# Grouping the small products of two scans by the part of the array they use

## The chip, the cores and the metric

One core of one Trainium2 chip runs the whole program in one launch. The metric is device time in microseconds (us), the median of several executions. The profile is one more execution, taken by the hardware profiler. Engines are called PE (TensorE's matmuls), PEld (its weight loads), DVE (VectorE), ACT (ScalarE), POOL (GpSimd) and SP (SyncE, which issues the transfers).

## The reference

Three layers run one after the other on a sequence of 2048 tokens with 1024 features, all in float32. Each of the first two projects its input, runs a chunked linear attention with four heads, multiplies by gates, projects back and normalises. Only the attention of these two layers is touched by the change.

```python
# layer 0, chunks of 64 tokens, 4 heads, dk = 64, dv = 128
scores = jnp.einsum('bnihd,bnjhd->bnhij', q_dec, k_dec)
scores = jnp.where(causal, scores, 0.0)
o_intra = jnp.einsum('bnhij,bnjhe->bnihe', scores, v)
chunk_state = jnp.einsum('bnjhd,bnjhe->bnhde', k_state, v)
s_in = _chunk_scan(decay, chunk_state)      # S_n = decay * S_{n-1} + chunk_state
o_inter = jnp.einsum('bnihd,bnhde->bnihe', q_dec, s_in)
return o_intra + o_inter
# layer 1, chunks of 128 tokens, the same with fixed decays per head
```

The third layer (a gated delta rule and a sparse attention) takes more than half of the time and is the same in both kernels.

## The kernel before

The sequence is worked in two halves of 1024 tokens, first both halves of layer 0, then both of layer 1, then layer 2. A half has eight tiles of 128 tokens (`NTI`). In each half a scan goes over the eight tiles (`loop` in `layer0` and in `layer1`). It is woven with a projection (`run_T`, whose products are L199 and L210 with output `pj`): `weave` takes the next step of whichever stream is behind, and a scheduler then sets the final order on each engine by what is ready. So PE works on long projections of 128x512, and small products of the scan stand among them in clumps.

For each tile the scan makes two PSUM tiles, both called `m` in the trace (two buffers, tag `m2`):

- `su`, the scores and the chunk states. In layer 0 these are four score products (L491, 64 rows by 128 columns of the array, two heads per 128 partitions) and eight state products (L497, 64 by 64, one for each chunk, head pair and head). In layer 1 four score products (L781, 64 by 128) and four state products (L787, 128 by 64).
- `o`, the output. Each head first takes masked scores times values (L516 or L802, over the whole 128 by 128 array), and on top of it queries times the state that entered the chunk: two products of 64 by 64 in layer 0 (L519), one of 64 by 128 in layer 1 (L803).

A float32 product is issued as two passes, so one product is two records in the trace. After `su` DVE masks the scores into `sm` (L498) or `rsm` (L788) and advances the state (L504; L791 and L793). After `o` the function `head_norm` normalises (ACT, DVE, POOL, DVE in layer 0), and its `turn`, run later, transposes the result back on PE (L601) and multiplies it into the gates (L602).

The order inside a clump is the order of the code: in the output head by head, the whole-array product and then the products over parts.

Of the kernel before, what the change touches and what calls it, by code (L numbers as in the profile page):

```python
# [22 lines left out]
P = 128  # L23
# [5 lines left out]
NTI = HALF // P  # L29
# [32 lines left out]
class Builder:  # L62
# [275 lines left out]
    def layer0(self, src, dst):  # L338
        nc, A = self.nc, self.A
# [42 lines left out]
        for h in range(self.NH):  # L382
# [16 lines left out]
            eb, en, ed, dk = [], [], [], []  # L399
# [63 lines left out]
            kst = [self.slot("kst").rearrange("p (j c) -> p j c", j=4) for _ in range(NTB)]  # L463
# [11 lines left out]
            vs = [self.slot("v") for _ in range(NTI // 2)]  # L475
            def ev(cb, ti, ps):
                nc.scalar.copy(vs[ti // 2].rearrange("p (a c) -> p a c", a=2)[:, ti % 2, :], ps)
            self.cols_N(w_in, 512, 512, xh, xl, ev)

            def loop(S):  # L480
                turn = None
                for ti in range(NTI):
                    sl = slice(ti * P, (ti + 1) * P)
                    v = vs[ti // 2].rearrange("p (a h e) -> p a h e", a=2, h=4)[:, ti % 2]
                    sm = sms[ti % 2]

                    su = self.psum("m2").rearrange("p r (b x) -> p r b x", b=4)
                    for hb in range(2):
                        for q in range(2):
                            r = slice(64 * q, 64 * q + 64)  # L490
                            nc.tensor.matmul(su[:, q, hb, :], en[hb][r, sl], eb[hb][r, sl], start=True, stop=True)  # L491
                    for hb in range(2):
                        for q in range(2):
                            for c in range(2):
                                cr, r = slice(64 * c, 64 * c + 64), slice(64 * q, 64 * q + 64)
                                hd = 2 * hb + q
                                nc.tensor.matmul(su[r, c, 2 + hb, :], kst[ti // 4][cr, ti % 4, hd * 64:hd * 64 + 64], v[cr, hd, :], start=True, stop=True)  # L497
                    nc.vector.copy_predicated(sm.rearrange("p (b q) i -> p q b i", q=2), cmask[:, None, None, :].to_broadcast([P, 2, 2, P]),  # L498
                                              su[:, :, 0:2, :])
                    Ss = [S]  # L500
                    for c in range(2):
                        Sn = self.small([P, 2, P], "glaS", bufs=4)
                        for q in range(2):
                            nc.vector.scalar_tensor_tensor(out=Sn[:, q, :], in0=S[:, q, :], scalar=dk[q][:, 2 * ti + c:2 * ti + c + 1],  # L504
                                                           in1=su[:, c, 2 + q, :], op0=ALU.mult, op1=ALU.add)
                        S = Sn
                        Ss.append(S)
                    yield
                    if turn:
                        turn()  # L510
                    yield
                    o = self.psum("m2")[:, :, :256].rearrange("p q (b e) -> p q b e", b=2)
                    for hb in range(2):
                        for q in range(2):
                            r, hd = slice(64 * q, 64 * q + 64), 2 * hb + q
                            nc.tensor.matmul(o[:, q, hb, :], sm[:, hd, :], v[:, hd, :], start=True, stop=False)  # L516
                            for c in range(2):
                                cr = slice(64 * c, 64 * c + 64)
                                nc.tensor.matmul(o[cr, q, hb, :], eb[hb][r, ti * P + 64 * c:ti * P + 64 * c + 64], Ss[c][r, hb, :], start=False, stop=True)  # L519
                    turn = self.head_norm(o, mixA, sl, center=False)  # L520
                    yield
                turn()
                self.glaS = S
# [3 lines left out]
            def ev(cb, tb, ps):  # L527
                nc.scalar.activation(mixB[:, cb, tb * TB:(tb + 1) * TB], ps, AF.Silu)
            self.weave((loop(S), 4 * NTI + 6), (self.run_T(w_in, self.jobs(2576, 512, ev), xh, xl), 64))
            S = self.glaS  # L530
            if h == 0:
# [161 lines left out]
    def layer1(self, src, dst, rot):  # L693
        nc, A = self.nc, self.A
# [3 lines left out]
        for t, n in ((cos, 0), (sin, 1)):  # L698
# [17 lines left out]
                                compare_op=ALU.is_ge, fill=0.0)  # L716
        R = self.small([P, 2, P], "retS", bufs=3)
        nc.vector.memset(R, 0.0)
        hist = []
# [5 lines left out]
        for h in range(self.NH):  # L725
# [14 lines left out]
            kN = [self.slot("kN").rearrange("p (j c) -> p j c", j=4) for _ in range(NTB)]  # L740

            qkT = [[self.slot("qkT").rearrange("p (s t) -> p s t", s=2) for _ in range(NTB)] for _ in range(2)]
# [23 lines left out]
            vs = [self.slot("v") for _ in range(NTI // 2)]  # L766
            def ev(cb, ti, ps):
                nc.scalar.copy(vs[ti // 2].rearrange("p (a c) -> p a c", a=2)[:, ti % 2, :], ps)
            self.cols_N(w_in, 512, 512, xh, xl, ev)

            def loop(R):
                turn = None
                for ti in range(NTI):
                    sl = slice(ti * P, (ti + 1) * P)
                    so = slice(ti % 4 * P, (ti % 4 + 1) * P)
                    v = vs[ti // 2].rearrange("p (a h e) -> p a h e", a=2, h=4)[:, ti % 2]
                    su = self.psum("m2").rearrange("p r (b x) -> p r b x", b=4)
                    for hb in range(2):
                        for q in range(2):
                            r = slice(64 * q, 64 * q + 64)  # L780
                            nc.tensor.matmul(su[:, q, hb, :], qkT[hb][ti // 4][r, 1, so], qkT[hb][ti // 4][r, 0, so], start=True, stop=True)  # L781
                    sm = self.small([P, 4, P], "rsm", tag="t512", bufs=4)
                    yield
                    for hb in range(2):
                        for q in range(2):
                            r, hd = slice(64 * q, 64 * q + 64), 2 * hb + q
                            nc.tensor.matmul(su[r, 0, 2 + hb, :], kN[ti // 4][:, ti % 4, hd * 64:hd * 64 + 64], v[:, hd, :], start=True, stop=True)  # L787
                    nc.vector.tensor_tensor(out=sm.rearrange("p (b q) i -> p q b i", q=2), in0=su[:, :, 0:2, :],  # L788
                                            in1=cm[:, None, None, :].to_broadcast([P, 2, 2, P]), op=ALU.mult)
                    Rn = self.small([P, 2, P], "retS", bufs=3)  # L790
                    nc.vector.tensor_tensor(out=Rn, in0=su[:, 0, 2:4, :], in1=R, op=ALU.add)  # L791
                    for b in range(2):
                        nc.vector.tensor_scalar(out=Rn[:, b, :], in0=Rn[:, b, :], scalar1=gam[:, b:b + 1], scalar2=None, op0=ALU.mult)  # L793
                    yield
                    if turn:
                        turn()
                    yield
                    o = self.psum("m2")[:, :, :256].rearrange("p q (b e) -> p q b e", b=2)
                    for hb in range(2):
                        for q in range(2):  # L800
                            r, hd = slice(64 * q, 64 * q + 64), 2 * hb + q
                            nc.tensor.matmul(o[:, q, hb, :], sm[:, hd, :], v[:, hd, :], start=True, stop=False)  # L802
                            nc.tensor.matmul(o[:, q, hb, :], qkT[hb][ti // 4][r, 0, so], R[r, hb, :], start=False, stop=True)  # L803
                    R = Rn
                    turn = self.head_norm(o, mixA, sl, center=True)
                    yield
                turn()
                self.retR = R

            mixA = mixes["mixA"]  # L810
            gates = self.jobs(2048, 512, partial(gate, "mixB", psc))
            self.weave((loop(R), 4 * NTI + 6), (self.run_T(w_in, gates[1:], xh, xl), 48))
            R, mixB = self.retR, mixes["mixB"]

# [1261 lines left out]
```

## Time and profile before

| what | value |
|---|---|
| device time, median of 3 executions | 3320.11 us (3312.62 to 3323.88) |
| the profiled execution | 3313.21 us, its span 3311.5 us |
| PE busy | 3156.6 us, 95% |
| DVE, ACT, POOL busy | 1906.7, 1195.7 and 1072.0 us |

The span is the time between first and last instruction; the 1.7 us between the two numbers lie around it. In a row of the timeline stand the start, the length and the number of equal instructions merged into one row. Matmuls overlap in the pipeline, so a length is longer than the step to the next one: what a pass costs is read from differences of starts. A form such as 64\*128 after the names tells how many rows and columns of the array a product uses.

### The profile page before, as it was taken

What the parts mean: (1) busy time and instruction counts of PE and PEld (TensorE: products, weight loads), DVE (VectorE), ACT (ScalarE), POOL (GpSimd) and SP (SyncE); (2) the same over time, 40 slices, a digit from 0 to 9 for tenths busy, and PEclk for the clock granted to TensorE, in tenths of its full rate; (3) what the DMA queues carried; (4) which work ended last, traced back from release to release, by engine and by line L of the source; (5) the groups of instructions that cost most, each with busy time, mean ns of one, the idle gap of its engine ahead of it and who ended that gap; (6) DMA issues with size and microseconds to landing.
All of it is one profiled execution on the core that took longest, in us unless ns stands there. A gap on an engine that the chain in (4) does not pass through costs nothing. (4 is left out here: it accounts for less than half of the span.)

```text
span 3311.5 us, 45462 instructions
## 1 busy us (share of the span) xinstructions
PE 3156.6 (95%) x16546; PEld 2600.4 (79%) x16546; DVE 1906.7 (58%) x4954; ACT 1195.7 (36%) x1991; POOL 1072.0 (32%) x905
## 2 busy tenths in 40 slices
PE   8999999999999999999899899989998799998899
PEld 5778877778878788877787878779776698876787
DVE  2226455246513653165558657876588775798863
ACT  4222243112322223222333524444353452553552
POOL 4123362223563537352311211612026121125111
PEclk9999999999999999999999999999999899999999
DMA  4112245107345536253467655564545524435422
GB/s 123 38 45 96 97 132 168 59 27 276 125 133 166 184 124 203 76 198 114 154 214 232 192 195 185 174 189 141 191 147 157 175 83 175 162 119 177 129 58 74
DMA packets 380743, 472.24 MB, mean 143 GB/s; under 512 B 81251, under 2 KB 268851, under 8 KB 380502
## 3 DMA queue, kind: packets, MB, share of 16 engines
q1 hardware_dynamic: 380502, 469.20, 43.5%
q8 instruction: 130, 2.13, 0.3%
q14 instruction: 111, 0.91, 0.1%
HBM read 365.13 MB, written 103.99 MB: 142 GB/s over the span
## 5 line engine op out<-in xcount | busy, mean ns | idle before, releaser
L144 POOL TENSOR_TENSOR wl<-wr,wh 128x1024 fp32r<-128x1024 f32 x126 | 302.2, 2403 | 541.5 <-ACT wh L143 531.9
L199 PE MATMUL pj<-xh,wh 128*128 128x512 f32 x992 | 396.4, 400 | 8.6 <-ACT wh L143 4.1
L210 PE MATMUL pj<-wh,xh 128*128 128x512 f32 x1024 | 401.3, 394 | 1.7 <-DVE t L749 0.7
L210 PE MATMUL pj<-wl,xh 128*128 128x512 f32 x1024 | 401.7, 392 | 1.2 <-POOL wl L144 1.1
L210 PE MATMUL pj<-wh,xl 128*128 128x512 f32 x1024 | 399.9, 391 | 0.0
L199 PE MATMUL pj<-xl,wh 128*128 128x512 f32 x992 | 394.9, 398 | 0.0
L199 PE MATMUL pj<-xh,wl 128*128 128x512 f32 x992 | 391.3, 394 | 0.0
L1211 PE MATMUL pj<-xh,wh 128*128 128x512 f32 x896 | 368.3, 411 | 8.2 <-ACT spl L1238 6.4
L1211 PE MATMUL pj<-xl,wh 128*128 128x512 f32 x896 | 361.1, 403 | 7.2 <-DVE xl L1144 6.7
L1211 PE MATMUL pj<-xh,wl 128*128 128x512 f32 x896 | 359.7, 401 | 0.0
L143 ACT CAST wh<-wr 128x1024 fp32r<-128x1024 f32 x126 | 130.6, 1038 | 443.5 <-PE pj L199 135.2
L199 PEld LDWEIGHTS pj<-xh,wh 128*128 128x128 f32 x992 | 182.7, 184 | 62.0 <-issue 7.2
L210 PEld LDWEIGHTS pj<-wh,xh 128*128 128x128 f32 x1024 | 192.3, 188 | 45.6 <-issue 2.0
L210 PEld LDWEIGHTS pj<-wl,xh 128*128 128x128 f32 x1024 | 192.4, 188 | 42.5 <-POOL wl L144 3.4
L210 PEld LDWEIGHTS pj<-wh,xl 128*128 128x128 f32 x1024 | 192.3, 188 | 39.3 <-issue 0.2
L199 PEld LDWEIGHTS pj<-xh,wl 128*128 128x128 f32 x992 | 182.6, 184 | 46.6 <-issue 4.4
L199 PEld LDWEIGHTS pj<-xl,wh 128*128 128x128 f32 x992 | 182.7, 184 | 46.0 <-issue 5.3
L1211 PEld LDWEIGHTS pj<-xh,wh 128*128 128x128 f32 x896 | 174.5, 195 | 46.5 <-ACT spl L1238 8.8
L1372 DVE SCALAR_TENSOR_TENSOR score<-relu,iwc,score 128x512 f32<-128x512 f32 (+3 forms) x266 | 189.4, 712 | 32.8 <-ACT relu L1371 29.9
L1211 PEld LDWEIGHTS pj<-xl,wh 128*128 128x128 f32 x896 | 174.5, 195 | 42.7 <-DVE xl L1144 9.9
L1211 PEld LDWEIGHTS pj<-xh,wl 128*128 128x128 f32 x896 | 174.0, 194 | 39.5
L1668 PE MATMUL mm<-PT,ckvN 128*128 128x128 f32 x1088 | 147.3, 276 | 4.6 <-ACT PT L1663 4.6
(564 smaller groups left out, 6369.3 us busy)
## 6 DMA issues: line engine op xcount, KB each, us to landing
wh<-kh SPq DMA_DIRECT2D x140, 512.0 KB, 4.0
wl<-kl SPq DMA_DIRECT2D x140, 512.0 KB, 5.0
wr<-in_l_w_in_dram SPq DMA_DIRECT2D x92, 512.0 KB, 3.7
kh<-wh SPq DMA_DIRECT2D x37, 512.0 KB, 3.2
kl<-wl SPq DMA_DIRECT2D x37, 512.0 KB, 4.4
wr<-in_l_w_out_dram SPq DMA_DIRECT2D x32, 512.0 KB, 3.6
x<-y SPq DMA_DIRECT2D x32, 512.0 KB, 2.6
wr<-in_w_in_dram SPq DMA_DIRECT2D x29, 512.0 KB, 4.5
```

Of the source, the lines that this page charges most:

```text
L143: nc.scalar.copy(wh, raw)
L144: nc.gpsimd.tensor_tensor(out=wl, in0=raw, in1=f(wh), op=ALU.subtract)
L199: self.nc.tensor.matmul(ps[:m, :], a[:, k, :], b[tb][k], start=(n == 0), stop=(n == 3 * KT - 1))
L210: self.nc.tensor.matmul(ps, a[tb][k][:, o:o + P], b[:, k % 2, :], start=(n == 0), stop=(n == 3 * KT - 1))
L1211: nc.tensor.matmul(ps, a[:, k, :], b[0][k], start=k + n == 0, stop=k == KT - 1 and n == 2)
L1372: nc.vector.scalar_tensor_tensor(out=o, in0=t[:, :m], scalar=w, in1=o, op0=ALU.mult, op1=ALU.add)
L1668: nc.tensor.matmul(oT[:, h * P:(h + 1) * P], ckvN[:, k0 + k, :], pt[:, k * P:(k + 1) * P], start=k0 + k == 0, stop=k0 + k == i)
```

## The change

In the output all four whole-array products now come first, and then all products over parts. The scores and states of the next tile are issued right behind the output in the code (a function `scores`), ahead of `head_norm`; in layer 0 the states come first in it and the scores second, in layer 1 the other way round. The start flag stands on the first of the two heads that share a bank. The number of instructions is the same.

```diff
+            def scores(ti):
+
+                v, sl = values(ti), slice(ti * P, (ti + 1) * P)
+                su = self.psum("m2").rearrange("p r (b x) -> p r b x", b=4)
+                for hb in range(2):
+                    for q in range(2):
+                        for c in range(2):
...
+                            nc.tensor.matmul(su[r, c, 2 + hb, :], kst[ti // 4][cr, ti % 4, hd * 64:hd * 64 + 64], v[cr, hd, :], start=True, stop=True)
+                for hb in range(2):
+                    for q in range(2):
+                        r = slice(64 * q, 64 * q + 64)
+                        nc.tensor.matmul(su[:, q, hb, :], en[hb][r, sl], eb[hb][r, sl], start=True, stop=True)
+                return su
...
                     for hb in range(2):
                         for q in range(2):
-                            r, hd = slice(64 * q, 64 * q + 64), 2 * hb + q
-                            nc.tensor.matmul(o[:, q, hb, :], sm[:, hd, :], v[:, hd, :], start=True, stop=False)
+                            nc.tensor.matmul(o[:, q, hb, :], sm[:, 2 * hb + q, :], v[:, 2 * hb + q, :], start=hb == 0, stop=False)
+                    for hb in range(2):
+                        for q in range(2):
                             for c in range(2):
-                                cr = slice(64 * c, 64 * c + 64)
-                                nc.tensor.matmul(o[cr, q, hb, :], eb[hb][r, ti * P + 64 * c:ti * P + 64 * c + 64], Ss[c][r, hb, :], start=False, stop=True)
+                                cr, r = slice(64 * c, 64 * c + 64), slice(64 * q, 64 * q + 64)
+                                nc.tensor.matmul(o[cr, q, hb, :], eb[hb][r, ti * P + 64 * c:ti * P + 64 * c + 64], Ss[c][r, hb, :],
+                                                 start=False, stop=hb == 1)
+                    if ti < NTI - 1:
+                        su = scores(ti + 1)
                     turn = self.head_norm(o, mixA, sl, center=False)
...
@@ -796,12 +816,17 @@
                     for hb in range(2):
                         for q in range(2):
-                            r, hd = slice(64 * q, 64 * q + 64), 2 * hb + q
-                            nc.tensor.matmul(o[:, q, hb, :], sm[:, hd, :], v[:, hd, :], start=True, stop=False)
-                            nc.tensor.matmul(o[:, q, hb, :], qkT[hb][ti // 4][r, 0, so], R[r, hb, :], start=False, stop=True)
+                            nc.tensor.matmul(o[:, q, hb, :], sm[:, 2 * hb + q, :], v[:, 2 * hb + q, :], start=hb == 0, stop=False)
+                    for hb in range(2):
+                        for q in range(2):
+                            r = slice(64 * q, 64 * q + 64)
+                            nc.tensor.matmul(o[:, q, hb, :], qkT[hb][ti // 4][r, 0, so], R[r, hb, :], start=False, stop=hb == 1)
                     R = Rn
+                    if ti < NTI - 1:
+                        su = scores(ti + 1)
```

The order that comes of it on PE, first in the scan of layer 0: its second output (`m_137`) and the scores and states of its third tile. Before:

```order
L601 MATMUL tp_1201<-ident,on_1165 128x128 x4
L516 MATMUL m_137_1215<-v_868,sm_178 128x128
L519 MATMUL m_137_1215<-glaS_1137,eb_480 64x128
L519 MATMUL m_137_1215<-glaS_1189,eb_480 64x128
...
L516 MATMUL m_137_1215<-v_868,sm_178 128x128
L519 MATMUL m_137_1215<-glaS_1137,eb_585 64x128
L519 MATMUL m_137_1215<-glaS_1189,eb_585 64x128
L491 MATMUL m_140_1238<-eb_480,en_481 128x128 x2
L491 MATMUL m_140_1238<-eb_585,en_586 128x128 x2
L497 MATMUL m_140_1238<-v_869,kst_722 64x128 x8
L199 MATMUL pj_1326<-xh,wl_1112 128x512
```

And the same place after the change (L523 is the whole-array product, L528 the one over a part, L491 the states and L495 the scores):

```order
L613 MATMUL tp_1201<-ident,on_1178 128x128 x4
L523 MATMUL m_137_1215<-v_868,sm_178 128x128 x4
L528 MATMUL m_137_1215<-glaS_1137,eb_480 64x128
L528 MATMUL m_137_1215<-glaS_1189,eb_480 64x128
...
L528 MATMUL m_137_1215<-glaS_1137,eb_585 64x128
L528 MATMUL m_137_1215<-glaS_1189,eb_585 64x128
L491 MATMUL m_138_1228<-v_869,kst_722 64x128 x8
L495 MATMUL m_138_1228<-eb_480,en_481 128x128 x2
L495 MATMUL m_138_1228<-eb_585,en_586 128x128 x2
L199 MATMUL pj_1326<-xh,wh_1111 128x512
```

The clump holds the same products; four alternations became one, and states and scores changed places. The next clump stands as many projections later as before, give or take one.

In layer 1 the first output (`m_955`) and the second tile's scores on PE, before:

```order
L199 MATMUL pj_7362<-xh,wh_7250 128x512
L802 MATMUL m_955_7292<-v_7013,rsm_7270 128x128
L803 MATMUL m_955_7292<-retS_6315,qkT_6657 128x128
...
L802 MATMUL m_955_7292<-v_7013,rsm_7270 128x128
L803 MATMUL m_955_7292<-retS_6315,qkT_6659 128x128
L781 MATMUL m_960_7322<-qkT_6657 128x128 x2
L781 MATMUL m_960_7322<-qkT_6659 128x128 x2
L787 MATMUL m_960_7322<-v_7013,kN_6655 64x128 x4
L199 MATMUL pj_7362<-xl,wh_7250 128x512
```

And after the change (L822, L826, L792 and L796 are the same four lines):

```order
L199 MATMUL pj_7362<-xh,wh_7250 128x512
L822 MATMUL m_955_7292<-v_7013,rsm_7274 128x128 x4
L826 MATMUL m_955_7292<-retS_6315,qkT_6657 128x128 x2
L826 MATMUL m_955_7292<-retS_6315,qkT_6659 128x128 x2
L792 MATMUL m_956_7301<-qkT_6657 128x128 x2
L792 MATMUL m_956_7301<-qkT_6659 128x128 x2
L796 MATMUL m_956_7301<-v_7013,kN_6655 64x128 x4
L199 MATMUL pj_7362<-xl,wh_7250 128x512
```

Here too the scores followed the output directly before, and only the alternation inside the output went.

Last, a place on PE well ahead of the scan of layer 0, in the projection of the keys, where one score product of the first tile stood alone (rows with - are of before; `m_126` is the first tile's `su`):

```order
 L199 MATMUL pj_769<-xl,wh_725 128x512
 L199 MATMUL pj_769<-xh,wl_726 128x512
-L491 MATMUL m_126_1120<-eb_480,en_481 128x128
 L472 MATMUL tp_763<-ident,z_406 128x128 x4
 L199 MATMUL pj_802<-xh,wh_731 128x512
```

It joins the other score products of that tile, which now wait for the states that stand ahead of them. Each half of layer 0 has two such places (the second place of the second half holds two products). On POOL nothing moved; on SP and ACT some neighbours changed places.

## Rows read from the trace of the kernel before

**Rows 1.** The page, busy time by engine (share of the span, instructions).

```profile
PE 3156.6 (95%) x16546; PEld 2600.4 (79%) x16546; DVE 1906.7 (58%) x4954; ACT 1195.7 (36%) x1991; POOL 1072.0 (32%) x905
```

**Rows 2.** PE by windows, the four scans, then layer 2: length, busy, clock, DMA.

```profile
183.00:272.00 89.00, 89.00 (x631) 1.00 0.17 48
...
sum 378.00, PE 378.00; mean PE 94.50
...
1520.00:3311.00 1791.00, 1660.07 (x9139) 0.97 0.48 156
```

**Rows 3.** Waits of PE from 120 to 1520: total us, times, longest.

```profile
PE pj L199 <- DVE eb L461: 2.1, 2, 1.1
...
PE pj L210 <- POOL wl L144: 1.1, 2, 0.7
```

**Rows 4.** Timeline of PE, a tile of layer 0: start, length, line, names.

```profile
200.43 0.60 PE L601 MATMUL tp<-ident,on 128*128 128x128 f32 x4
200.86 0.39 PE L516 MATMUL m<-v,sm 128*128 128x128 f32 x2
201.18 0.43 PE L519 MATMUL m<-glaS,eb 64*64 64x128 f32 x4
201.54 0.49 PE L516 MATMUL m<-v,sm 128*128 128x128 f32 x2
...
203.53 0.44 PE L519 MATMUL m<-glaS,eb 64*64 64x128 f32 x4
203.90 0.71 PE L491 MATMUL m<-eb,en 64*128 64x128 f32 x8
204.54 0.67 PE L497 MATMUL m<-v,kst 64*64 64x128 f32 x16
...
205.47 0.39 PE L199 MATMUL pj<-xh,wh 128*128 128x512 f32 x1
205.70 0.40 PE L199 MATMUL pj<-xl,wh 128*128 128x512 f32 x1
```

**Rows 5.** Timeline of PE, a tile of layer 1.

```profile
1036.88 0.38 PE L802 MATMUL m<-v,rsm 128*128 128x128 f32 x2
1037.19 0.48 PE L803 MATMUL m<-retS,qkT 64*128 64x128 f32 x2
1037.61 0.49 PE L802 MATMUL m<-v,rsm 128*128 128x128 f32 x2
...
1039.69 0.37 PE L803 MATMUL m<-retS,qkT 64*128 64x128 f32 x1
1039.70 0.37 PE L781 MATMUL m<-qkT 64*128 64x128 f32 x1
...
1040.56 0.66 PE L787 MATMUL m<-v,kN 128*64 128x128 f32 x8
...
1041.48 0.40 PE L199 MATMUL pj<-xh,wl 128*128 128x512 f32 x1
```

**Rows 6.** Timeline of PE, four whole-array products of the spatial gating together.

```profile
353.24 1.05 PE L549 MATMUL tp<-wsT,sv 128*128 128x128 f32 x8
354.04 0.48 PE L199 MATMUL pj<-xh,wh 128*128 128x512 f32 x1
```

**Rows 7.** Lines of PEld from 120 to 1520, the loads of these: busy, mean ns.

```profile
L549 PEld LDWEIGHTS tp<-wsT,sv 128*128 128x128 f32 x128 | 16.8, 191 | 1.3
```

**Rows 8.** Timeline of PE, a score product that stands alone.

```profile
125.09 0.39 PE L199 MATMUL pj<-xh,wl 128*128 128x512 f32 x1
125.41 0.48 PE L491 MATMUL m<-eb,en 64*128 64x128 f32 x2
125.83 0.66 PE L472 MATMUL tp<-ident,z 128*128 128x128 f32 x4
```

**Rows 9.** Timeline of ACT and DVE, `head_norm` of the output that ends at 192.7.

```profile
192.81 0.60 ACT L593 ACTIVATE on<-m 128x512 f32<-128x512 f32 x1 [0.84 <-PE m L519]
...
195.49 0.69 DVE L596 TENSOR_TENSOR on<-m,hnr 128x512 f32<-128x512 f32 x1
```

More of the change, by code (lines that the diff above doesn't have):

```diff
@@ L478, in layer0 @@
             self.cols_N(w_in, 512, 512, xh, xl, ev)
+            values = lambda ti: vs[ti // 2].rearrange("p (a h e) -> p a h e", a=2, h=4)[:, ti % 2]
+            def scores(ti):
[5 more added lines that the diff above has]
+                            cr, r = slice(64 * c, 64 * c + 64), slice(64 * q, 64 * q + 64)
+                            hd = 2 * hb + q
+                            nc.tensor.matmul(su[r, c, 2 + hb, :], kst[ti // 4][cr, ti % 4, hd * 64:hd * 64 + 64], v[cr, hd, :], start=True, stop=True)
[4 more added lines that the diff above has]
+                return su
             def loop(S):
                 turn = None
+                su = scores(0)
                 for ti in range(NTI):
                     sl = slice(ti * P, (ti + 1) * P)
-                    v = vs[ti // 2].rearrange("p (a h e) -> p a h e", a=2, h=4)[:, ti % 2]
+                    v = values(ti)
                     sm = sms[ti % 2]
[L487 to L497, printed above, removed]
                     nc.vector.copy_predicated(sm.rearrange("p (b q) i -> p q b i", q=2), cmask[:, None, None, :].to_broadcast([P, 2, 2, P]),
@@ L514, in loop @@
                         for q in range(2):
-                            r, hd = slice(64 * q, 64 * q + 64), 2 * hb + q
-                            nc.tensor.matmul(o[:, q, hb, :], sm[:, hd, :], v[:, hd, :], start=True, stop=False)
+                            nc.tensor.matmul(o[:, q, hb, :], sm[:, 2 * hb + q, :], v[:, 2 * hb + q, :], start=hb == 0, stop=False)
+                    for hb in range(2):
+                        for q in range(2):
                             for c in range(2):
-                                cr = slice(64 * c, 64 * c + 64)
-                                nc.tensor.matmul(o[cr, q, hb, :], eb[hb][r, ti * P + 64 * c:ti * P + 64 * c + 64], Ss[c][r, hb, :], start=False, stop=True)
+                                cr, r = slice(64 * c, 64 * c + 64), slice(64 * q, 64 * q + 64)
+                                nc.tensor.matmul(o[cr, q, hb, :], eb[hb][r, ti * P + 64 * c:ti * P + 64 * c + 64], Ss[c][r, hb, :],
+                                                 start=False, stop=hb == 1)
+                    if ti < NTI - 1:
+                        su = scores(ti + 1)
                     turn = self.head_norm(o, mixA, sl, center=False)
@@ L769, in layer1, with scores @@
             self.cols_N(w_in, 512, 512, xh, xl, ev)
+            values = lambda ti: vs[ti // 2].rearrange("p (a h e) -> p a h e", a=2, h=4)[:, ti % 2]
+            def scores(ti):
+                v, so = values(ti), slice(ti % 4 * P, (ti % 4 + 1) * P)
+                su = self.psum("m2").rearrange("p r (b x) -> p r b x", b=4)
+                for hb in range(2):
+                    for q in range(2):
+                        r = slice(64 * q, 64 * q + 64)
+                        nc.tensor.matmul(su[:, q, hb, :], qkT[hb][ti // 4][r, 1, so], qkT[hb][ti // 4][r, 0, so], start=True, stop=True)
+                for hb in range(2):
+                    for q in range(2):
+                        r, hd = slice(64 * q, 64 * q + 64), 2 * hb + q
+                        nc.tensor.matmul(su[r, 0, 2 + hb, :], kN[ti // 4][:, ti % 4, hd * 64:hd * 64 + 64], v[:, hd, :], start=True, stop=True)
+                return su
             def loop(R):
                 turn = None
+                su = scores(0)
                 for ti in range(NTI):
@@ L775, in loop @@
                     so = slice(ti % 4 * P, (ti % 4 + 1) * P)
[L776 to L781, printed above, removed]
+                    v = values(ti)
                     sm = self.small([P, 4, P], "rsm", tag="t512", bufs=4)
                     yield
-                    for hb in range(2):
-                        for q in range(2):
-                            r, hd = slice(64 * q, 64 * q + 64), 2 * hb + q
-                            nc.tensor.matmul(su[r, 0, 2 + hb, :], kN[ti // 4][:, ti % 4, hd * 64:hd * 64 + 64], v[:, hd, :], start=True, stop=True)
                     nc.vector.tensor_tensor(out=sm.rearrange("p (b q) i -> p q b i", q=2), in0=su[:, :, 0:2, :],
@@ L800, in loop @@
                         for q in range(2):
-                            r, hd = slice(64 * q, 64 * q + 64), 2 * hb + q
-                            nc.tensor.matmul(o[:, q, hb, :], sm[:, hd, :], v[:, hd, :], start=True, stop=False)
-                            nc.tensor.matmul(o[:, q, hb, :], qkT[hb][ti // 4][r, 0, so], R[r, hb, :], start=False, stop=True)
+                            nc.tensor.matmul(o[:, q, hb, :], sm[:, 2 * hb + q, :], v[:, 2 * hb + q, :], start=hb == 0, stop=False)
+                    for hb in range(2):
+                        for q in range(2):
+                            r = slice(64 * q, 64 * q + 64)
+                            nc.tensor.matmul(o[:, q, hb, :], qkT[hb][ti // 4][r, 0, so], R[r, hb, :], start=False, stop=hb == 1)
                     R = Rn
+                    if ti < NTI - 1:
+                        su = scores(ti + 1)
                     turn = self.head_norm(o, mixA, sl, center=True)
```

## The prediction

> **What bounds the kernel now.** I read the page's busy times first, then the windows of the four scans, then the waits of PE, then the timeline of single tiles. The page says that PE is busy for 95% of the span [rows 1]. A busy PE need not be a fast PE, so the question is whether it ever stands still around the change, and what the steps between its passes are. In the windows of the four scans PE is busy for 378.0 of 378.0 us, and the granted clock in the first is 1.00, the upper level of 2.4 GHz [rows 2]. In the waits from 120 to 1520 us, which holds all four scans, the longest entry is 2.1 us in total, and waits for a low weight part come to 1.1 us [rows 3]. So PE's own chain of passes sets the time here, and whatever shortens that chain moves all that follows.
>
> The timeline shows what a pass costs in which company.
>
> - Four products over the whole array standing together (L549) are 8 passes in a row of 1.05 us. The last pass alone lasts 0.27, so the first to the last start is 0.78 and the step 0.11; the next projection starts 0.80 behind the first of them [rows 6].
> - In the output of layer 0 one whole-array product is two passes. From its first start at 200.86 to the first product over a part at 201.18 are 0.32: one step of 0.11 and 0.21 for the passage to parts [rows 4]. Behind the parts the whole-array product at 201.54 is 0.49 long, 0.28 of it the last pass, so its second pass starts 0.21 behind the first instead of 0.11 [rows 4]. A passage thus costs at both ends.
> - 16 passes over 64 by 64 parts (L497, together) last 0.67, the last one 0.27 of it: 0.40 from first to last start [rows 4]. They run four abreast, on four different parts, in four steps, the first of 0.16 and the next ones of about 0.11. The same kind of product in the output runs only two abreast, since each head meets one half of the array's rows.
>
> **The change part by part.** I set the tile of before against one built from these steps.
>
> Layer 0, a tile with scores behind it. Before: from the first output product at 200.86 to the second projection at 205.47, less the ordinary step of 0.23 between projections (205.47 to 205.70), 4.38 us [rows 4]. After, from the first start on:
>
> 1. four whole-array products, 7 steps of 0.11: 0.78 [rows 6];
> 2. passage to parts 0.21: 0.99;
> 3. eight products over parts, now four abreast as in L497: 0.40, so 1.39;
> 4. eight state products in the same form and hence without a passage, four more steps of 0.11: 1.83;
> 5. passage 0.20, then the scores as before, 0.64 from 203.90 to 204.54 with the passage behind them [rows 4]: 2.67;
> 6. the first projection is followed late, at 0.33 instead of 0.23 (in before the 0.93 from 204.54 to 205.47 hold it): 0.11, so 2.78.
>
> The saving is 1.60 us a tile. There are 7 such tiles in each half, so 14 x 1.60 = 22.4. The last tile of a half has no scores: before 203.53 - 200.86 = 2.67, then 0.37 for the parts and 0.11, 3.15 together; after 0.99 + 0.40 + 0.20 + 0.11 = 1.70; saving 1.45, times 2 is 2.9. A score product that stood alone goes too: 125.09 to 125.83 is 0.74 where an ordinary step takes 0.23, so 0.51 [rows 8]. Two such places in a half cost 1.02, and adding these products to the first tile's scores costs two steps of 0.11: 0.8 a half, 1.6 in all. Layer 0: 26.9 us.
>
> Layer 1, a tile with scores. Before: 1041.48 - 0.23 - 1036.88 = 4.37 [rows 5]. After: 0.78 for the whole-array products, 0.21 for the passage, 0.44 for four products of 64 by 128 (the length of the scores in layer 0, 0.64 less the passage of 0.20), four pairs of score passes in the same form 0.45, passage 0.20, and then states, passage and slow projection as before, 1041.48 - 1040.56 - 0.23 = 0.69 [rows 5]. Sum 2.77, saving 1.60, times 14 is 22.4. In the last tile: before 1039.69 - 1036.88 = 2.81, 0.42 for its two passes and the passage out, and 0.11, 3.34 together; after 0.78 + 0.21 + 0.44 + 0.20 + 0.11 = 1.74; 1.60 twice is 3.2. Layer 1: 25.6 us.
>
> Together 52.5 us. The steps of 0.11 for products of different rows and banks side by side are read off L497 and L549, not off the output itself, since before never has it so; that is the one unknown. Its lower end is that accumulating products run one at a time, its upper end what I took; the rivals price the former.
>
> What I set at nothing. The number of instructions and DVE's, ACT's and POOL's work stay. DVE's mask waits for the clump's end as before, with scores and states changing places. Weights: PE waits 1.1 us for low parts in 1400 us [rows 3], and each weight block serves 48 projections of 0.23, 10.9 us, besides the clumps; taking 1.6 us from each clump leaves this cover. The normalisation behind an output runs from 192.81 to 195.49 + 0.69 = 196.18, and its transposes start at 200.43 [rows 4, 9]: 4.2 us of cover. The distance from output to transposes changes by some 0.2 us, since the scores, states and about as many projections still lie between. Were it gone, every tile would wait for what is lacking; a normalisation 4 us longer would have to come first. `su` and `o` keep their own of the two PSUM buffers, so no new wait for one arises.
>
> **A rule against it.** In the trace four whole-array products in a row keep the step of 0.11 although each load of their weights lasts 191 ns [rows 6, 7]. The Trainium skill, "TensorE: Matmul & The Clock Gate", Part 3, says that a weight load overlaps running matmuls only when it goes to another group of rows; by its figures of P / 1.2 ns for a load of P columns (107 ns for 128) and 128 / 2.4 (53 ns) for a pass I estimate a step of 0.16 us, and 0.05 x 8 x 32 tiles = 13 us less gain. The trace doesn't agree: the step of 0.11 holds over all 8 passes. What would follow if `sm` and `v` behaved otherwise is the first rival, priced from rows.
>
> **The rivals.**
>
> *Products of the same place don't pipeline.* If the six later whole-array passes of a tile step by 0.21, as the second pass behind a passage does [rows 4], rather than 0.11, the loss is 6 x 0.10 x 32 = 19 us. L549 speaks against it [rows 6]; for it, only that `sm` and `v` are other operands. Time 3283. Chance 8%.
>
> *Accumulating products on both row halves run one by one.* New is that products which add to a bank stand beside such products of the other row half. If each pass then has to leave the array first, at 0.21, a tile of layer 1 has 8 x 0.21 = 1.68 in place of 0.44, and one of layer 0 16 x 0.21 = 3.36 in place of 0.40. That is 16 x (1.24 + 2.96) = 67 us, 14 more than the gain: 3331, slower. It turns the sign when a pass costs 53 / 384 = 0.14 us more than I took (384 passes). Against it: at 1039.69 an accumulating pass of the output and at 1039.70 a score pass, on the other row half, start side by side [rows 5]. Chance 5%.
>
> *The gain is given back.* A shorter scan could bring a weight, a transfer or a chain of the third layer forward as the next bound. For it: in the 1791 us from 1520 on PE is idle for 131 [rows 2], so other things end last there. Against it: that layer starts from the second one's rows, which PE makes, so its idle stretches move along. If a third to all is lost, 3282 to 3317. Chance 8%.
>
> *More than reckoned*, from passages around transposes that I left out: below 3252, chance 4%.
>
> **How the numbers follow.** The profiled execution takes 3313.2, its span 3311.5 with 1.7 around it; less 52.5 it is 3260.7. That execution lies 6.9 below the median of the three runs; the middle of all four times is 3316.7 (between 3313.21 and 3320.11), and I take the gain from there: 3264. The forecast has a chance of 75%, with a range of its own of 3255 to 3275 from the spread of the runs and some 5 us in the steps. Adding the cases on both sides until about two in ten are out gives 3252 to 3284. A change of less than 0.3%, some 10 us, can't be told from none here. Faster by more: the forecast, the first rival, the larger gain and most of the third, 0.92; same 0.03; slower 0.05.
>
> **What would show it.** The profile after should have the four whole-array products as one row of 8, about 1.05 long; the parts and states of layer 0 as 16 and 16 passes, together about 1.1 long; 3.0 us from the first output product to the second projection where 4.6 stood; PE's busy time near 3104, and its idle time unchanged at 3311.5 - 3156.6, some 155 [rows 1]. Wrong it is if passes inside a group step by 0.2, if a new wait stands ahead of the transposes or a projection, or if the third layer starts earlier and ends as late as before.

## The result, and the profile after

The changed kernel takes 3277.99 us (median of four, 3270.99 to 3280.16) beside 3318.53 for the kernel before (3312.62 to 3323.88): a ratio of 0.9878, 95% interval 0.9866 to 0.989. Forecast were 3264 with a range of 3252 to 3284. The gain is 40.5 us where 52.5 were added up.

The first thing to look at is the tile that the prediction built from steps. The timeline of PE, a tile of layer 0 after the change (start in us, length, engine, line, names; it answers to [rows 4]):

```profile
198.48 0.60 PE L613 MATMUL tp<-ident,on 128*128 128x128 f32 x4
198.91 1.06 PE L523 MATMUL m<-v,sm 128*128 128x128 f32 x8
199.90 0.67 PE L528 MATMUL m<-glaS,eb 64*64 64x128 f32 x16
200.38 0.62 PE L491 MATMUL m<-v,kst 64*64 64x128 f32 x16
200.93 0.71 PE L495 MATMUL m<-eb,en 64*128 64x128 f32 x8
201.58 0.50 PE L199 MATMUL pj<-xh,wh 128*128 128x512 f32 x1
201.92 0.40 PE L199 MATMUL pj<-xl,wh 128*128 128x512 f32 x1
202.16 0.40 PE L199 MATMUL pj<-xh,wl 128*128 128x512 f32 x1
```

From the first output product to the second projection, less an ordinary step, are 201.92 - 0.23 - 198.91 = 2.78 us: the tile as built. The whole-array row is 1.06 long, the output's parts 0.67, as L497 was in [rows 4]. In layer 1 (answers to [rows 5]):

```profile
1013.52 1.05 PE L822 MATMUL m<-v,rsm 128*128 128x128 f32 x8
1014.50 0.71 PE L826 MATMUL m<-retS,qkT 64*128 64x128 f32 x8
1015.05 0.61 PE L792 MATMUL m<-qkT 64*128 64x128 f32 x8
1015.59 0.66 PE L796 MATMUL m<-v,kN 128*64 128x128 f32 x8
1016.18 0.50 PE L199 MATMUL pj<-xl,wh 128*128 128x512 f32 x1
1016.51 0.40 PE L199 MATMUL pj<-xh,wl 128*128 128x512 f32 x1
```

Here 1016.51 - 0.23 - 1013.52 = 2.76, where 2.77 was built. So the tiles are as short as forecast, and yet 12 us are missing. The page's row for PE (busy us, share, instructions; [rows 1] has 3156.6) and the windows of the four scans and of layer 2 (length, PE busy, instructions, granted clock, DMA share, GB/s; answers to [rows 2]) say where to look:

```profile
PE 3108.9 (95%) x16546; PEld 2576.7 (79%) x16546; DVE 1915.7 (58%) x4954; ACT 1194.6 (36%) x1991; POOL 1070.1 (33%) x905
```

```profile
181.00:266.50 85.50, 85.50 (x676) 1.00 0.18 50
608.00:679.00 71.00, 71.00 (x553) 1.00 0.22 66
1012.00:1110.00 98.00, 94.89 (x570) 1.00 0.71 232
1370.00:1470.00 100.00, 96.55 (x583) 1.00 0.61 203
1486.00:3278.00 1792.00, 1657.48 (x9140) 0.97 0.48 156
```

PE is still never idle in the two scans of layer 0. In those of layer 1 it now stands idle, for 3.11 and 3.45 us, where before it was busy throughout. In all it is idle for 3278.4 - 3108.9 = 169.5 us instead of 154.9. The waits of PE name the newcomer (engine, tile and line, what it waited for: total us, times, longest; 120 to 1490 us, answers to [rows 3]):

```profile
PE tp L613 <- DVE on L592: 6.0, 4, 3.1
PE tp L188 <- DVE xl L165: 3.2, 1, 3.2
PE pj L210 <- POOL wl L144: 2.3, 2, 2.0
```

The first does not exist before: the transposes of the normalised output `on` now wait for DVE. The table shows what each stage gave. A shift is the start of a projection in the kernel before minus the start of the same projection (counted from the first) in the run, worked out from the two timelines; a stage's gain is the change of the shift over it. The stages are cut at the projections that the kernel before starts at 120, 315, 531, 740, 1014, 1187, 1382 and 1552 us; from 315 to 531 the changed kernel gains nothing (all in us, one profiled execution each).

| run | layer 0 scan 1 | scan 2 | rest of layer 0 | layer 1 scan 1 | between | scan 2 |
|---|---|---|---|---|---|---|
| forecast | 13.45 | 13.45 | 0 | 12.8 | 0 | 12.8 |
| changed kernel | 13.5 | 13.1 | -3.6 | 7.6 | -4.8 | 8.3 |
| the same, another execution | 13.5 | 13.0 | -0.4 | 6.4 | -0.8 | 7.5 |
| layer 0 alone changed | 13.4 | 12.8 | 0.1 | 0.0 | -1.1 | 0.0 |
| layer 1 alone changed | 0.0 | 0.1 | -0.6 | 6.0 | -1.0 | 7.7 |
| layer 1 without side jobs | 13.5 | 13.0 | 1.5 | 12.8 | 1.8 | 12.8 |
| last version (early2) | 13.4 | 7.2 | 1.8 | 12.6 | 1.9 | 12.7 |

Layer 0 gave what was added up. Layer 1's scans gave 15.9 and 13.9 of 25.6.

What holds `on` is in DVE's timeline (start, length, names, and in brackets the idle time before it and what ended it). The changed kernel in the second scan of layer 1; first the end of an output on PE, then DVE, then the transpose on PE:

```profile
1421.73 0.71 PE L826 MATMUL m<-retS,qkT 64*128 64x128 f32 x8
```

```profile
1423.26 1.47 DVE L981 TENSOR_TENSOR wl<-wr,wh 128x1024 fp32r<-128x1024 f32 x1
...
1425.26 0.87 DVE L587 BATCH_NORM_STATS2 n4st<-m 128x6 f32<-128x128 f32 x4
...
1426.44 0.17 DVE L130 TENSOR_SCALAR n4r<-n4mv 128x4 f32<-128x4 f32 x1
1431.12 1.23 DVE L981 TENSOR_TENSOR wl<-wr,wh 128x1024 fp32r<-128x1024 f32 x1 [4.51 <-DMA kl<-wl]
1432.26 1.36 DVE L592 TENSOR_SCALAR on<-m,n4mv,n4r 128x128 f32<-128x128 f32 x4
```

```profile
1432.72 0.33 PE L613 MATMUL tp<-ident,on 128*128 128x128 f32 x1 [3.13 <-DVE on L592]
```

And the kernel before in a tile of the same layer, which the prediction does not use:

```profile
1090.57 0.89 DVE L575 BATCH_NORM_STATS2 n4st<-m 128x6 f32<-128x128 f32 x4 [1.94 <-PE m L803]
...
1091.77 0.17 DVE L130 TENSOR_SCALAR n4r<-n4mv 128x4 f32<-128x4 f32 x1
1092.95 1.23 DVE L956 TENSOR_TENSOR wl<-wr,wh 128x1024 fp32r<-128x1024 f32 x1 [1.01 <-DMA kl<-wl]
1094.09 1.36 DVE L580 TENSOR_SCALAR on<-m,n4mv,n4r 128x128 f32<-128x128 f32 x4
```

```profile
1097.55 0.27 PE L601 MATMUL tp<-ident,on 128*128 128x128 f32 x1
```

In layer 1's scans a side job prepares weights of layer 2: it loads `wr`, ACT rounds it to `wh`, DVE forms the rest `wl = wr - wh`, and both go out by DMA (`kh<-wh`, `kl<-wl`). These subtractions stand in DVE's queue among the steps of the normalisation, and a subtraction that waits for the store of an earlier `wl` keeps what stands behind it waiting too.

In the tile of before, the statistics start when PE has finished the output. One subtraction stands ahead of `on`, which is finished at 1094.09 + 1.36 = 1095.45, 4.9 us behind the output; the transposes start at 1097.55. So the cover, the time from finished `on` to its first transpose, is 2.1 us there, not the 4.2 read off layer 0. In the tile of after, the output ends at 1421.73 + 0.71 = 1422.44. One subtraction stands ahead of the statistics and another ahead of `on`, which stood 4.51 us for a store. `on` is finished at 1433.62, 11.2 us behind the output, and PE stood 3.13 us for it.

All 16 tiles of layer 1, worked out from the timelines in the same way (mean us in scan 1 and scan 2):

| run | from the output's end to finished `on` | from the output's end to the first transpose |
|---|---|---|
| kernel before | 5.4 and 4.9 | 8.2 and 8.2 |
| changed kernel | 8.5 and 8.1 | 8.8 and 8.8 |
| the same, another execution | 8.1 and 8.3 | 8.8 and 8.9 |
| layer 1 without side jobs | 4.3 and 4.3 | 7.4 and 7.4 |

So PE does not come to its transposes sooner after an output than before. It is the normalisation that comes about 3 us later, and that takes the cover, 3.2 us in the median tile of layer 1 before and 0.5 in the shortest. The waits of DVE for that store tripled (980 to 1490 us; total, times, longest; before, then after; the other execution has 18.9 in total):

```profile
DVE wl L956 <- DMA kl<-wl: 5.4, 3, 3.1
```

```profile
DVE wl L981 <- DMA kl<-wl: 16.4, 6, 4.5
```

The jobs hardly became faster with PE. From the first to the last of a scan's 12 and 10 subtractions are 80.5 and 64.9 us before, 76.5 and 63.8 after: about 7 us a job either way. What sets this pace is not shown. PE's idle time holds 6.6 of the 9.7 us that the two scans lack; the rest stands in its busy time, and that it is waits shorter than the overlap of two passes is a reading, not shown.

### The profile page after: what moved, and what is told of

It reads as the page before. It is cut to its first block, busy times and chain, and to the rows that moved or that the text cites. A ratio compares the mean times of both kernels' runs of the same rounds, so it can differ in the third digit from the quotient of the medians.

```text
span 3278.4 us, 45462 instructions
## 1 busy us (share of the span) xinstructions
PE 3108.9 (95%) x16546; PEld 2576.7 (79%) x16546; DVE 1915.7 (58%) x4954; ACT 1194.6 (36%) x1991; POOL 1070.1 (33%) x905
## 5 line engine op out<-in xcount | busy, mean ns | idle before, releaser
L1236 PEld LDWEIGHTS pj<-xh,wl 128*128 128x128 f32 x896 | 173.2, 193 | 39.2
```

Of the source, the lines that this page charges most:

```text
L1236: nc.tensor.matmul(ps, a[:, k, :], b[0][k], start=k + n == 0, stop=k == KT - 1 and n == 2)
```

## The experiments

All times are medians with their range, the number of runs in brackets; ratios are to the kernel before in the same session.

**Each layer alone.** The kernel before with the changed `layer0` (l0_only), or the changed `layer1` (l1_only), and nothing else.

> The change in layer 0 alone, layer 1 as before. Theory (passages cost what the steps say, and a later wait takes some back): its two scans shorten by 13.4 us each, and some 3.5 are lost at the end of layer 0, where the projection out starts on split gates that DVE has not finished; total about 23 us, ratio 0.993. Rival (that loss was a chance of one execution): 26.5 us, ratio 0.992. In the trace the first projection of the third layer should stand 23 or 26.5 us earlier.

> The change in layer 1 alone, layer 0 as before. Theory (the shorter tile uncovers the wait of the transposes for the normalised output): its two scans give 7.7 and 8.4 us instead of 12.8 each, and some 4 us go at the start of layer 1's second half; total 11 to 16 us. Rival (the waits came from layer 0's shift, which moved transfers against the scan): 25 us, no wait ahead of the transposes.

l0_only: 3288.71 (3285.36 to 3289.06, 5), ratio 0.9912 [0.9898, 0.9925], 28.2 us less than the 3316.88 before. l1_only: 3306.18 (3300.63 to 3309.9, 6), 0.9964 [0.9952, 0.9977], 10.7 less. Together 38.9, as good as the 40.5 of both. The loss sits in layer 1; layer 0's gain arrives, 24.2 us of it at the end of the span in the profile. The 3.5 us that the expectation for l0_only put at the end of layer 0 were not lost there (the stage has 0.1), so its rival held.

**What the grouping is made of.** In `half` the parts directly follow each pair's whole-array products, so that a tile has two passages more; `regroup` is the kernel before with its output products grouped and the scores left where they were.

```diff
 half, against the changed kernel, in both layers
                     for hb in range(2):
                         for q in range(2):
                             nc.tensor.matmul(o[:, q, hb, :], sm[:, 2 * hb + q, :], ...
-                    for hb in range(2):
                         for q in range(2):
                             (the products over parts)
```

> The change with two alternations in an output instead of one (both whole-array products of a head pair, then their products over parts, then the next pair). Theory: every passage costs the same, so a tile of layer 0 takes 0.37 us more than after the change and one of layer 1 0.40; the clumps grow by 5.9 and 6.4 us in all. Where the transposes of layer 1 wait, the growth of its clumps is hidden in their wait: 3284 to 3287. Rival (no wait counts, all adds up): 3290. If grouping as such and not the number of passages counts, it is as fast as the change or as slow as before.

> Only the output regrouped; scores and states stand in the code where and in the order they stood before. Theory: in layer 0 one passage more per tile with scores (0.16 us net, 2.2 in all), and the lone score products stay (1.6): 3.8 us more than after the change, 3282. Rival (the scores placed behind the output carry a good part of the gain): 3300 or more.

A tile of layer 0 in `half`, and one in `regroup` (timeline of PE):

```profile
197.75 0.61 PE L523 MATMUL m<-v,sm 128*128 128x128 f32 x4
198.29 0.45 PE L527 MATMUL m<-glaS,eb 64*64 64x128 f32 x8
198.67 0.71 PE L523 MATMUL m<-v,sm 128*128 128x128 f32 x4
199.31 0.45 PE L527 MATMUL m<-glaS,eb 64*64 64x128 f32 x8
...
201.11 0.40 PE L199 MATMUL pj<-xl,wh 128*128 128x512 f32 x1
```

```profile
199.70 1.06 PE L515 MATMUL m<-v,sm 128*128 128x128 f32 x8
200.69 0.67 PE L520 MATMUL m<-glaS,eb 64*64 64x128 f32 x16
201.28 0.72 PE L491 MATMUL m<-eb,en 64*128 64x128 f32 x8
201.93 0.67 PE L497 MATMUL m<-v,kst 64*64 64x128 f32 x16
...
202.86 0.39 PE L199 MATMUL pj<-xh,wh 128*128 128x512 f32 x1
```

Measured the same way, `half` needs 201.11 - 0.23 - 197.75 = 3.13 us and `regroup` 2.93, where the changed kernel needs 2.78 and the kernel before 4.38. Two passages cost 0.35, some 0.17 each. The grouping of the outputs makes 1.45 of the 1.60 us; putting the states behind the output's parts makes the last 0.15. In the scans of layer 0 `half` gained 10.8 and 10.7, `regroup` 11.6 and 11.8. The medians, 3279.85 (3277.53 to 3284.3, 4; 0.9889 [0.9873, 0.9906]) and 3279.83 (3279.18 to 3285.62, 4; 0.9893 [0.9877, 0.9909]), are too close to the changed kernel's for whole times to show such differences. Both kernels came out faster than their expectations of 3284 to 3287 and 3282. In layer 1 `regroup` has the changed kernel's tile of 2.77, and gained 6.3 and 7.5. `half` has 3.16, by its starts, 6.2 us more in 16 tiles, and yet it gained 5.8 and 7.4, 13.2 beside the 13.7 to 15.9 of the short tile: there something other than PE sets the pace.

**Side jobs moved out of the scan.** Theory: the side subtractions hold `on`. Rivals: `head_norm` itself is too slow, or PE's order. In after_nosplit, and in the kernel before as its control, no side job is issued inside the scan, and twice as many behind it.

```diff
+            self.spare = 0
             self.weave((loop(R), 4 * NTI + 6), (self.run_T(w_in, gates[1:], xh, xl), 48))
+            self.spare = 2
...
+            self.spare = 1
             self.residual_ln(mixA, mixB, A["l1_w_out"], ...
```

> The changed kernel, with the side jobs of layer 1 (each splits a weight block of the third layer: a load, a cast on ACT, a subtraction on DVE, two stores) taken out of its scans and put into the projection behind them. Theory A (in the scans these subtractions wait on DVE for a store, and the normalisation of the output stands behind them in DVE's queue): no wait ahead of the transposes, each scan of layer 1 gives 12.8 us against before instead of 5 to 8, and the third layer starts 5 to 10 us earlier than after the change, unless the moved jobs cost as much where they now stand. Rival B (the normalisation is too long for the shorter tile by itself): the waits ahead of the transposes stay at some 9 us in all and the scans give 7 to 8.

> The kernel before, with the side jobs of layer 1 moved in the same way. Both theories: its scans gain nothing, since PE never waited in them; the time shows what the moved jobs cost in the projection behind, 0 to 8 us. Theory A: the changed kernel with moved jobs is faster than this by 50 us or more.

after_nosplit: 3272.9 (3271.32 to 3278.73, 4), 0.9864 [0.9848, 0.9881]. The kernel before with the same edit: 3317.24 (3309.36 to 3325.33, 12), 0.9995 [0.9984, 1.0005], no change. By whole times after_nosplit can't be told from the changed kernel either (0.9878, and 0.9862 in another session), and the 44.3 us between the two runs miss the 50 expected; the waits and the stages tell more. Waits for `on` fell to 0.2 us on PE and 0.7 on its weight loads, from 6.0 and 9.1, and the second scan of layer 1 gained 12.7. In the first the shift rose by 9 us, but 3.3 of these were left at 1161 us and 3.6 more went before the second scan: at the end of the first scan and behind it PE waited 2.0 us for L848 (ACT) and 3.4 for L870 (DVE), which it does not in the changed kernel. The edit is less clean than meant: the scheduler pulled moved jobs forward, so that 15 subtractions start in the first scan, where the changed kernel has 12, and PE waited only 0.2 us for `on`. So what counts is where they stand and how long they wait, not their number.

**Another buffer for `wl`.** If the wait for the store is the whole cause, a sixth `wl` buffer (and one `gladk` less, to make room) should cure it.

```diff
-        self.pools(ctx, "a", {"pj": 2, "tp": 2, "m2": 2}, NTB, dict(wr=2, wh=5, wl=5))
+        self.pools(ctx, "a", {"pj": 2, "tp": 2, "m2": 2}, NTB, dict(wr=2, wh=5, wl=6))
...
-                d = self.small([P, HALF // 64], "gladk", bufs=4)
+                d = self.small([P, HALF // 64], "gladk", bufs=3)
```

> The changed kernel with six buffers for low weight parts instead of five (and three instead of four for a small table of layer 0, to make room). Theory A: a subtraction then finds a free buffer one store earlier, most waits of DVE for a store go, and each scan of layer 1 gives 10 to 12.8 us; 5 to 9 us faster than the change. Rival B: no difference.

> The kernel before with the same six buffers: no difference from before by either theory (0 to 2 us), since PE never waits for a normalisation there.

after_wl6: 3282.82 (3280.0 to 3285.15, 4), 0.9887 [0.9871, 0.9903]; before_wl6: 3325.49 (3318.68 to 3333.65, 12), 1.0022 [1.0013, 1.0032]. No cure. The waits of PE and DVE in after_wl6, from 120 and from 980 to 1490 us:

```profile
PE tp L613 <- DVE on L592: 4.0, 3, 1.8
```

```profile
DVE wl L981 <- ACT wh L980: 132.1, 22, 40.9
```

The subtraction no longer waits for a store but for its `wh`, 22 times instead of 16 in the changed kernel, and `on` still waits behind it; the scans of layer 1 gained 5.8 and 9.9. The store was only one of several things that the side job waits for; what hurts is that a waiting job stands ahead of `on`. Both kernels with this edit lose in layer 2 in their profiles, before_wl6 5.6 us and after_wl6 10.3, and the control is 0.2% slower where no difference was expected. Why stays open.

**No side jobs at all.** `spare = 0` for the whole of layer 1. The weights are then made behind the layer, which costs a long tail, so only its scans are compared.

```diff
-            b.spare = 1
+            b.spare = 0
             b.layer1(x1, x2, rot)
```

> The changed kernel with no side job in the whole of layer 1: the weight splits that are left run behind it, as a tail between layers 1 and 2. Only the scans of layer 1 are to be compared. Theory A (side subtractions on DVE, which wait for their loads and stores, hold up the normalisation queued behind them): no wait ahead of the transposes, each scan 12.8 us shorter than before. Rival B (the normalisation is too long for the shorter tile): waits of 4 us a scan stay, the scans gain 7 to 9. The whole is slower than the change by the tail, some tens of us; that says nothing on either.

The whole run takes 3389.03 us (one execution), beside 3318.71 before. Its windows of layer 1's two scans (columns as above), and DVE in one tile:

```profile
990.00:1110.00 120.00, 120.00 (x687) 1.00 0.23 75
1340.00:1450.00 110.00, 110.00 (x647) 1.00 0.16 48
```

```profile
1021.75 0.17 DVE L130 TENSOR_SCALAR n4r<-n4mv 128x4 f32<-128x4 f32 x1
1023.08 1.37 DVE L592 TENSOR_SCALAR on<-m,n4mv,n4r 128x128 f32<-128x128 f32 x4 [1.16 <-POOL n4r L133]
```

PE is busy throughout again, nothing on DVE stands between the statistics and `on`, and the scans gain 12.8 each, as forecast. So `head_norm` itself has cover enough, and the side jobs took layer 1's gain. The edit takes away their transfers and casts too; that they act by their place ahead of `on` is read from the waits of DVE and PE above.

**A version without the hold.** The jobs must go elsewhere than into layer 1's scans. `early` starts them in layer 0's first half; early2 lets layer 0's query and key projections issue them in both halves instead.

```diff
 early
-            self.spare = h
+            self.spare = 1
...
+            self.spare = 0
             self.weave((loop(R), 4 * NTI + 6), (self.run_T(w_in, gates[1:], xh, xl), 48))
+            self.spare = 1
 early2: the second part as above, and in place of the first, for q and for k
             def ev(cb, tb, ps):
-                if h:
-                    self.aside(2)
+                self.aside(2)
```

> The changed kernel with side jobs begun earlier: also one beside each projection step of layer 0's first half (12 of them), none woven into the scans of layer 1. By its order eight subtractions still fall into the first scan of layer 1 and two into the second. Theory A: the second scan gives 12 to 12.8 us and the first 8 to 11, and if layer 0's first half hides the twelve jobs, 3268 to 3272. Rival (transfers and DVE of layer 0's first half have no room): what layer 1 gains is lost there, 3278 or more.

> The changed kernel once more, beside the others on one chip: 3274 to 3282 us; in its trace the hold of some 3 us at the end of layer 0 is gone if it was a chance of one execution, and stays if the change makes it.

> The changed kernel with sixteen side jobs more in the key and query projections of layer 0's first half, where DVE is busy for 5.8 of 63 us before, and none woven into the scans of layer 1 (by its order eight subtractions still fall into the first of them, none into the second). Theory A: layer 0 keeps its 26 us, since these jobs end before its scan; the first scan of layer 1 gives 9 to 12 us, the second 12.8: 3260 to 3268. Rival: the early transfers hold up layer 0's first half as in the run that had them beside its later projections: 3268 or more.

early: 3268.59 (3265.46 to 3273.29, 5), 0.9848 [0.9835, 0.9862]; the changed kernel again: 3273.18 (3270.04 to 3275.23, 4), 0.9862 [0.9846, 0.9878]; early2: 3264.56 (3261.92 to 3266.71, 5), 0.9832 [0.9819, 0.9846]. Layer 1's scans gave 12.6 and 12.7 in both. In `early` the jobs now fell into layer 0's scans, which gave 9.5 and 10.1 with 6.1 us of waits ahead of their transposes: a hold like that of layer 1. In early2 PE waits for nothing in the scans of layer 1, and its list from 100 to 1500 us begins so:

```profile
PE pj L210 <- POOL wl L144: 4.6, 6, 1.2
PE tp L611 <- DVE on L606: 3.0, 2, 2.3
```

Both belong mostly to layer 0 (L606 is the last step of its normalisation), so the 26 us that the expectation let layer 0 keep were not kept. Some 5 us went in the projections ahead of the second scan, whose low weight parts now come late; that is most of what the stage of 7.2 in the table lacks. The 3.0 us stand in the second scan itself. Ahead of the longer of these two waits the job that waits is on ACT, in front of the first step of the normalisation (L603):

```profile
627.80 1.05 ACT L143 CAST wh<-wr 128x1024 fp32r<-128x1024 f32 x1 [6.93 <-DMA wr<-in_l_w_in_dram]
628.76 0.59 ACT L603 ACTIVATE on<-m 128x512 f32<-128x512 f32 x1
```

It is a cast of the layer's own weights, which waits for their load. Early2 is the fastest kernel seen, 55.1 us under the kernel before in its session, and its ratio lies below both of the changed kernel's (its interval ends where the repeat's begins).

## Why the prediction was right, and where it failed

- *What bounds the kernel.* Right: shortening PE's chain moved all that follows. Layer 0 alone is worth 28.2 us in the median, for 26.9 forecast and 13.4 + 12.8 = 26.2 by the stages of its profile.
- *The steps.* Right to a hundredth: 2.78 us a tile in layer 0, and 2.76 for 2.77 in layer 1. The one unknown, that accumulating products on different rows and banks run as L497 does, was as taken: 16 passes of the output's parts last 0.67.
- *The first two rivals* fell by the same rows. Had later whole-array passes stepped by 0.21, L523 would be 1.06 + 0.6 long; had accumulating products run singly, L528 would be above 3 us and not 0.67.
- *The rule against it.* The step of 0.11 holds with `sm` and `v` too. The Trainium skill ("TensorE: Matmul & The Clock Gate", Part 3) would let a weight load overlap only where it goes to other rows; the 1.06 us of L523 disagree with it as L549 did, since its loads last 192 ns each and its passes step by 0.11. The estimate of 0.16 us there took a load at 107 ns where [rows 7] has 191, so it was too mild a price for that rule.
- *"What I set at nothing"* failed in one term, the waits of DVE ahead of the normalisation. The time of a normalisation was read off one tile of layer 0 and taken for both layers and for after, though `head_norm` takes other steps in layer 1 (the statistics L575 on DVE where layer 0 squares on ACT). That the way from output to transposes changes little held: it is 8.2 us in layer 1 before, 8.8 after with the waits, 7.4 without side jobs. That DVE's work stays was true of the instructions, not of their waits: in layer 1 side subtractions stand among the steps, they kept their pace of about 7 us a job while PE's tiles became shorter, and `on` came 3 us later behind its output. "A normalisation 4 us longer would have to come first" names the condition that came near. The term of layer 1 was 25.6 and measured 15.9, 13.9 and 13.7 in three profiles (the changed kernel twice, l1_only), and 25.6 without side jobs. The prediction named the sign ("a new wait ahead of the transposes") and gave it no price.
- *"The gain is given back"*, the third rival, is true in part but in another place. It was expected in layer 2, which took only 0.7 and 1.0 us more in the two profiles of the changed kernel (in the variants' single profiles from 10.3 more to 2.6 less, so a few us there can't be told); the loss happens in the scans themselves.
- *Idle unchanged, PE busy near 3104.* Idle rose by 14.6 us; busy came to 3108.9. Of the 14.6, 6.6 are in layer 1's scans by the windows. The losses of 3.6 us at the end of layer 0 (`tp L188` waiting for `xl`) and of 4.8 between layer 1's scans are not fixed to the change: the repeat has 0.4 and 0.8 there, while `half` loses 4.2 in the first place, and before_wl6 and before_nosplit, whose outputs are not grouped, 2.8 and 3.2 in the second. What makes them come and go stays open. The profiled execution was also the slowest of its four.
- *Luck in the range.* The time lies within 3252 to 3284, but the upper end came from rivals that did not arrive. The forecast's own range of 3255 to 3275 misses 3277.99 by 3 us, and the loss that made the difference had no price in it.

By the repeat the stages come to 13.5 + 13.0 - 0.4 + 6.4 - 0.8 + 7.5 = 39.2, with 39.1 at the end of the span; in the median of its session the gain is 3318.71 - 3273.18 = 45.5, since the profiled execution of before lies 5.5 below that session's median and the repeat's 0.9 above its own.

## What to carry to other kernels

Before a stretch on the bounding engine is shortened, read the cover of each chain that feeds it in every layer where the change lies, not in one tile: the same helper, with other steps, had 4.2 us in one, and in the next 3.2 in the median tile and 0.5 in the shortest. Look at what stands ahead of that chain's steps in their engines' queues; a background job there that waits for a buffer or a load passes its wait on, and is invisible while there is cover. Ask too whether the background jobs can go faster when the stage does. If not, move them to a stage with slack, rather than give them one more buffer.

## What the runs showed of the hardware that was not expected

- Accumulating 64 by 64 products on four different parts step by about 0.11 us for four passes behind a first step of 0.16, no slower than products that don't accumulate: L528 and L491 have 16 passes each in 0.67 and 0.62.
- A change between whole-array and part products costs PE about 0.17 us beyond the steps, by `half` against the changed kernel (0.35 for two).
- A DVE instruction that reuses a buffer under a store waited 4.51 us for it in the tile shown, where DMA's share in the windows of the two scans was 0.71 and 0.61, beside 0.23 and 0.16 without the side jobs.
